# Packing one projection tile into TensorE's column halves, and moving some weight sums to another stage

## The chip, the cores and the metric

The kernel runs on one core of one Trainium2 chip. The metric is the device time of one execution in microseconds (us), as the median of several runs. Below, TensorE (PE in the profile) multiplies, with its weight loads shown as PEld; VectorE is DVE, ScalarE is ACT, GpSimd is POOL, and SyncE is SP, whose queue issues nearly all the transfers of this kernel.

## The reference

One layer of a hybrid encoder: 512 tokens, model width 2048, everything in fp32.

```python
xn = rmsnorm(h, norm_mix)
y  = xn @ w_in                       # 2048 -> 7472 columns
o_gdn  = gdn_group(y[..., :4112])    # 8 heads x 128, gated delta rule
o_rwkv = rwkv_group(y[..., 4112:])   # 16 heads x 64, RWKV-7
h = h + concat([o_gdn, o_rwkv]) @ w_out
h = h + cross_attention(rmsnorm(h), rmsnorm(mem), wq, wk, wv, wo)   # 4 heads, 256 memory tokens
h = h + square(relu(rmsnorm(h) @ w_up)) @ w_down                    # hidden width 8192
out = rmsnorm(h, norm_final)
```

The columns of w_in are mostly whole 128-column tiles. What is left over are small groups: 64 columns for the decay and 64 for the in-context rate of RWKV, 160 for its gate, and 8 + 8 for the decay and the write strength of the delta rule (a_dt and b). Of the gate's 160 columns 128 fill a tile; the other 32 and the 16 of a_dt and b come to 48.

## The kernel before

**Precision.** Most products are made three times at the fast fp32r rate: weight and activation are each split into a high and a low part (a cast on ScalarE, a subtraction on VectorE), and hi x hi, hi x lo and lo x hi are summed in PSUM. Small products of the two recurrences are plain fp32 matmuls, which the hardware runs in two passes; the trace shows each pass as a record.

**The stages.** (1) Projection: 59 tiles of 128 columns of w_in, each 16 blocks of the width, three products a block, 48 matmuls of 128x128 weights on 512 tokens. The raw x (xr) is loaded in 16 blocks into buffers that later serve the recurrences (gq, gk, gAq, gkt and so on), multiplied by the norm's gain and split into xhi and xlo. The division by the root mean square comes at eviction, as a factor rstd for each token: evict multiplies PSUM by rstd into one of four y buffers. Between the tiles the chains of the recurrences (rwkv and gdn, head after head), the memory's keys (kp) and their product with the query weights (kq) run. The products of this last step, KQd, go to DRAM. (2) Values and their product with the output weights (vp, vo). (3) The output projection (op) in a Strassen-like form with seven products for eight. (4) Scores: sixteen steps, two token-by-memory halves g of eight steps n2, each loading 512 KB of KQd into a ring of three buffers (kqr, tag wraw), splitting it (kqh, kql) and multiplying it with hh and hl, 24 matmuls a step. Then attention (at). (5) The MLP's up and down products, in the seven-product form as well.

**The sums.** The seven-product form of the down weights needs four sums of the four quadrants of each block, s1 to s4. They don't depend on the activations, so for 13 of the 16 (e, m) groups they are made beforehand, stored to DRAM (Sd) and later loaded like weights. Each piece is four loads from w_dm, four VectorE operations in place and four stores. presum writes one piece. Eight groups are made during the projection stage in pieces of 410 columns by a chain of low rank (ahead); what is left is made in pieces of 512 or 256 columns (remaining, leftover) during the up and down stages in whatever buffers are free.

**The order.** In stages 1 and 5 the order of every engine is written out by a planner in the kernel: chains (Python generators) yield operations; run() picks the one that can start first by the planner's own clocks (cost, start) with a penalty by the chain's rank, and issues it. A chain can also yield a condition such as after("rstd"); that holds the chain in the planner, not on the chip. cost() holds the estimated time of each form of operation. In the score stage the framework orders the instructions by its own estimate of when they are ready, and adds the semaphores everywhere.

**Where the change touches it.** The third tile, n = 2, holds the 32 gate columns, a_dt, 24 zeros, b and 56 zeros (layout, at the end of the file). Its weights are entries w = 4 and 5 of the list wq, each 512 KB, prepared by loader; projections() multiplies it through gemm_ and hands it to evict; rows() reads it: gate rows 0 to 31, a_dt from row 32, b from row 64, mixes it with the token before (shiftmix), and writes the rows that the delta rule needs into R, then to DRAM as Rd and, transposed, into RT. gdn(h) reads Rd. splits() frees the weight buffers of the two down groups whose sums are made in place.

Of the kernel before, what the change touches and what calls it, by code (L numbers as in the profile page):

```python
# [73 lines left out]
def build(tc, I, out):  # L74
# [136 lines left out]
    def cost(op):  # L211
        eng, nm, _, a, k, out, ins, _ = op
        n = out.free_size()
        if eng == "PE":
            l = ins[0]
            if l.dtype == F32R:
                return n * 0.417 + (13.3 if state["shape"] is None else 120.0)
            sh = (l.partition_size(), l.free_size())
            sw = 0 if state["shape"] == sh or sh == (128, 128) else 100
            if nm == "transpose":  # L220
                return sw + (110 if sh[0] > 64 else 40)
            if sh == (64, 64):
                return sw + (32 if op[5].tensor.name[:2] in ("ri", "gi", "pa", "pv", "pu", "pw", "pk", "po", "pp") else 59)
            if sh[0] < 128 and n == 512:
                return sw + 530
            return sw + (115 if sh[0] < 128 and n == 128 else 2 * max(n * 0.84, 114))
        if eng == "DVE":
            if nm == "memset":
                return 60 + 0.3 * n
            if nm == "tensor_scalar":  # L230
                return 210 + 0.45 * n
            if nm == "tensor_tensor_scan":
                return 90 + 2.2 * n
            return 190 + 1.05 * n if nm == "scalar_tensor_tensor" else 154 + 1.05 * n
        if eng == "ACT":
            need = {AF.Tanh: "e", AF.Ln: "l", AF.Exp: "e"}.get(a[2] if len(a) > 2 else None)
            return (140 + 0.885 * n + 80 * sum(isinstance(x, bass.AP) for x in k.values())
                    + (40 if len(a) > 2 else 0) + (1283 if need and need != state["table"] else 0))
        if eng == "POOL":
            return 116 + 0.75 * n if nm == "memset" else 235 + 2.3 * n  # L240
        return 100.0
# [143 lines left out]
    wq = [("w", I["w_in"][n][:, h * 1024:(h + 1) * 1024]) for h in range(2) for n in range(2)]  # L385
    for n in range(2, NIN):
        wq += [("s", mem4[j]) for j in range(4) if n == NSQ[j]]
        wq += [("w", I["w_in"][n][:, h * 1024:(h + 1) * 1024]) for h in range(2)]
    kpo = [(0, 0), (1, 0), (0, 1), (1, 1)] + [(n, h) for n in range(2, KD) for h in range(2)]
    INSITU = ((3, 0), (3, 1))  # L390
    PRE = ((3, 0, 0),)
# [29 lines left out]
    hk = [("w", I["wk"][n][:, h * 1024:(h + 1) * 1024]) for n, h in kpo]  # L421
    wq += hk[:1] + [("m", m) for m in mem4[:2]] + hk[1:]
    wq += [("w", I["wqT"][n][:, g * 1024:(g + 1) * 1024]) for n in range(KD) for g in range(2)]
    NKP, NKQ = 2 * NIN, 2 * NIN + 2 * KD
    raws, halves, used, whole, piece = {}, {}, set(), set(), {}

    def pieceload(i):
# [10 lines left out]
    def loader():  # L438
        w = nm = 0
        for i, (kind, _) in enumerate(wq):  # L440
            yield lambda: i in raws
            if kind == "w":
                if w in (2, 3):
                    hi, lo = (tile_of(pm, [P, 1024], F32R, t, f"w{t}", 1) for t in ("BK", "AR", "GA", "GB")[2 * w - 4:2 * w - 2])
                else:
                    prev = (w if w < 2 else w - 2) - NWS
                    if prev >= 0:
                        yield lambda: prev + 2 * (prev > 1) in used
                    hi, lo = halves[w] if w in piece else wsplit()
                if w in piece:  # L450
                    yield after("piece", w)
                    yield from split_(raws[i][:, 512:], hi[:, 512:], lo[:, 512:])
                else:
                    yield from split_(raws[i], hi, lo)
                    halves[w] = hi, lo
                whole.add(w)
                w += 1
            else:
                yield from (memory if nm >= 4 else squares)(nm % 4, raws[i])
                nm += 1  # L460
# [88 lines left out]
    def gemm_(pts, his, los, first, nk=KD, left=None):  # L549

        w = len(pts)
        for h in range(nk // 8):
# [15 lines left out]
            for j in range(w):  # L568
                used.add(first + h * w + j)

    khl = []

    def projections():
# [4 lines left out]
        for n in range(2, NIN):  # L578
# [7 lines left out]
            if n >= 4:  # L586
                yield after("py", n - 2)
            pt = psb(f"py{n}", "mm", 2)
            yield from gemm_([pt], xhi, xlo, 2 * n, left="x" if n == NIN - 1 else None)
            chain(evict(n, pt), 0)  # L590
        yield after("py", NIN - 2)
        kpt = {}
# [59 lines left out]
        yield SY.dma_start(KQd[i // 2][:, i % 2 * 512:i % 2 * 512 + 512], ybuf[b][:, 0:512])  # L652
        yfree.append(b)

    def shiftmix(n, mi, o):
        yield after("py", n)
        y = ybuf[ys[n]]
        yield AC.activation(o, y[:, 2:514], AF.Copy, scale=col("mu", mi))
        yield DV.scalar_tensor_tensor(out=o, in0=y[:, 3:515], scalar=omu[:, mi:mi + 1],
                                      in1=o, op0=ALU.mult, op1=ALU.add)  # L660
        yfree.append(ys.pop(n))


# [5 lines left out]
    def rows():  # L669
# [1 line left out]
        yield DV.memset(R, 0.0)  # L671
        rs128 = tl("bon")
        g8 = slice(32, 40)
        b8 = slice(64, 72)
        yield after("rstd")
        yield AC.activation(nA, col("alog"), AF.Exp)
        yield DV.tensor_scalar(out=nA, in0=nA, scalar1=-1.0, scalar2=None, op0=ALU.mult)
# [9 lines left out]
        yield DV.tensor_scalar(out=sg1, in0=sg1, scalar1=0.5, scalar2=0.5, op0=ALU.mult, op1=ALU.add)  # L687
        yield from split_(sg1, sgh, sgl)
        events.add(("lowrank",))
        yield from shiftmix(2, 2, y2)  # L690
        yield AC.activation(y2[0:32, :], y2[0:32, :], AF.Tanh, scale=0.5)
        yield AC.activation(R[b8, :], y2[b8, :], AF.Tanh, scale=0.5)
        yield DV.tensor_scalar(out=y2[0:32, :], in0=y2[0:32, :], scalar1=0.5, scalar2=0.5,
                               op0=ALU.mult, op1=ALU.add)

# [23 lines left out]
        for c in range(4):  # L719
            yield TE.transpose(pt[:, c * P:(c + 1) * P], R[:, c * P:(c + 1) * P], ident)  # L720
        yield SY.dma_start(Rd, R[32:96, :])
        yield DV.tensor_copy(RT, pt.rearrange("p (c a b) -> p c a b", a=4, b=32)[:, :, 1:4, 0:8])

    hA, hB = HALF = slice(0, 64), slice(64, 128)
    solving = []
# [366 lines left out]
    def gdn(h):  # L1092
# [34 lines left out]
        E, B = pre.pop(h) if h else tl("gE"), tl("gqd")  # L1127
        if h == 0:
            yield SL.dma_start(E, Rd[h:h + 1, :].broadcast_to([P, T]))
        yield SL.dma_start(B, Rd[32 + h:33 + h, :].broadcast_to([P, T]))  # L1130
        k_ = yield from conv(0, 1, "gk")
        EG = tl("gEG")
        yield AC.activation(EG, E, AF.Exp)
# [549 lines left out]
    def turned():  # L1683
        g, _, probs = turn.pop(0)
        for e in range(2):
            for mt in range(2):
# [4 lines left out]
                S.copy(phi[kk], pt)  # L1691
                V.tensor_tensor(out=plo[kk], in0=pt, in1=phi[kk].bitcast(F32), op=ALU.subtract)

    for g in range(2):
        banks = (("mm", 2), ("mg", 2), ("mg", 2), ("mm", 2)), (("scr", 1), ("scg", 1), ("mx", 2), ("mx", 2))
        pts = [psb(f"sc{g}_{t}", *banks[g][t]) for t in range(4)]
        for n2 in range(8):
# [3 lines left out]
                nc.sync.dma_start(raw[:, i * 512:(i + 1) * 512], KQd[2 * n2 + i][:, g * 512:(g + 1) * 512])  # L1701
            wh = pw.tile([P, 1024], F32R, tag="whi", name=f"kqh{cnt[0]}", bufs=NWS)
            wl = pw.tile([P, 1024], F32R, tag="wlo", name=f"kql{cnt[0]}", bufs=NWS)
            split(raw, wh, wl)
            if g == 0 and n2 < 6:
                second(2 * n2 + 4)
                second(2 * n2 + 5)
# [15 lines left out]
        if g == 1:  # L1723
            for n in range(2):
                begun.append((psb(f"at{n}", "mg"), *wload(VOd[0][:, :, n * P:(n + 1) * P])))
                attend(*begun[n], 0)
        turn.append((g, pts, []))
        if g == 1:
            for t in range(4):
# [203 lines left out]
    def splits():  # L1933
        for u in units:
            if u[0] == "d" and u[1:3] in INSITU and u[1:] not in PRE:
                for i, w in order_of(u):
                    for x in xs(u):
# [2 lines left out]
                        halves[u, i, x] = hl = yield from take(hfree)  # L1940
                        yield from cut(r, *hl)
                        events.add(("half", u, i, x))
                        if w not in (A11, "s2") and (w != A12 or u == units[-1]):
                            wfree.append(r)
                continue
# [422 lines left out]
def layout(inputs):  # L2368
# [8 lines left out]
    def tiles(w):  # L2377
# [6 lines left out]
    zero = lambda n: np.zeros((D, n), f)  # L2384
    o0 = r0 + 3 * GW
    blocks = [w[:, o0:o0 + 128], w[:, o0 + 128:o0 + 256],
              w[:, o0 + 256:o0 + 288], w[:, 4 * GW:4 * GW + 8], zero(24),
              w[:, 4 * GW + 8:4 * GW + 16], zero(56)]
    for j in range(8):
        s = slice(j * P, (j + 1) * P)  # L2390
        blocks += [w[:, r0:][:, s], w[:, r0 + GW:][:, s], w[:, r0 + 2 * GW:][:, s]]
        blocks += [w[:, i * GW:][:, s] for i in (1, 0, 2, 3)]
    d["w_in"] = tiles(np.concatenate(blocks, 1))

    prm = np.zeros((P, NPRM), f)

# [69 lines left out]
```

## Time and profile before

| | |
|---|---|
| median of 3 runs | 2888.71 us (2887.84 to 2888.92) |
| span of the profiled execution | 2890.0 us; the page gives no other time for it |
| TensorE busy | 2862.2 us, 99% of the span |
| VectorE busy | 2333.9 us, 81% |
| ScalarE busy | 1571.7 us, 54% |
| GpSimd busy | 214.7 us, 7% |
| read from and written to HBM | 443.45 MB and 106.31 MB |

Matmuls are pipelined, so the length of a matmul's record is its latency, not the time that it keeps the array. How long it keeps the array is seen from the start of one to the start of the next. In the views below, a row of the timeline gives the start, the length, the engine, the line of the kernel, the operation, out<-in by the program's names, the form and the count. A row of stages gives the stretch, its length, and for each engine the busy time with the number of instructions in brackets. A row of groups gives the busy time, the mean in ns, and the idle time of the engine before these instructions with what ended it. A row of waits gives who waited for whom, the total in us, how often, and the longest.

### The profile page before, as it was taken

The numbers are of one execution on the slowest core, as the hardware profiler recorded it, in microseconds if no ns is written. First come the engines' busy times: TensorE is split into PE (matmuls) and PEld (weight loads), VectorE is DVE, ScalarE is ACT, GpSimd is POOL, SyncE is SP. The second block draws the span as 40 slices with busy tenths as digits, with TensorE's granted clock in tenths as the row PEclk, the third lists the DMA queues.
The fourth block names the chain that finished last, engine by engine and source line by source line (L and its number), as shares of the span: only waits on it lengthen the run. The fifth ranks groups of instructions, "written<-read, shape, count | busy, mean of one in ns | idle before, by whom it ended". The sixth has DMA issues, their size and how long they took to land.

```text
span 2890.0 us, 49168 instructions
## 1 busy us (share of the span) xinstructions
PE 2862.2 (99%) x18794; PEld 2419.1 (84%) x18794; DVE 2333.9 (81%) x3559; ACT 1571.7 (54%) x2233; POOL 214.7 (7%) x539
## 2 busy tenths in 40 slices
PE   9999999999999999999999999999999999999998
PEld 7877887877877888889988888888888888888887
DVE  7787787787877877769956898899998878786888
ACT  6555555645656655664445556555555644454544
POOL 0213213213212100000000000000000000000000
PEclk9999999999999999999999999999999999999999
DMA  5656656657656788784422354666565878887733
GB/s 191 166 147 176 176 149 187 165 154 189 180 161 200 214 257 274 232 292 151 124 95 88 110 164 153 199 195 207 189 200 178 292 249 277 295 257 247 265 101 110
DMA packets 321212, 553.01 MB, mean 191 GB/s; under 512 B 101128, under 2 KB 188428, under 8 KB 320976
## 3 DMA queue, kind: packets, MB, share of 16 engines
q1 hardware_dynamic: 293584, 518.41, 58.7%
q10 hardware_dynamic: 27392, 31.46, 3.1%
q8 instruction: 147, 2.41, 0.3%
q14 instruction: 89, 0.73, 0.1%
HBM read 443.45 MB, written 106.31 MB: 190 GB/s over the span
## 4 chain that ended last, share of the span: by engine, by line
PE 94%; DMA 3%; DVE 1%; ACT 1%; issue 1%; ACTq 0%; SPq 0%; DVEq 0%
PE py L257 22%; PE mxu L257 12%; PE mgd L257 6%; PE mgu L257 6%; PE mxd L257 6%; PE op L122 6%; PE vp L122 3%; PE mmu L257 3%; PE sc L122 3%; PE at L122 3%; PE scrd L257 3%; PE scgd L257 3%; PE mmd L257 3%; PE kq L257 3%; PE kp L257 2%; DMA wraw<-in_wo 1%
## 5 line engine op out<-in xcount | busy, mean ns | idle before, releaser
L257 ACT CAST whi<-wraw 128x1024 fp32r<-128x1024 f32 (+1 forms) x365 | 382.8, 1049 | 370.1 <-PE py L257 138.7
L257 DVE TENSOR_TENSOR wlo<-wraw,whi 128x1024 fp32r<-128x1024 f32 (+1 forms) x365 | 446.8, 1224 | 90.0 <-ACT whi L257 82.5
L257 PE MATMUL py<-xhi,whi 128*128 128x512 f32 x928 | 373.9, 403 | 6.8 <-ACT xhi L257 6.8
L257 PE MATMUL py<-xhi,wlo 128*128 128x512 f32 x928 | 373.1, 402 | 0.0
L257 PE MATMUL py<-xlo,whi 128*128 128x512 f32 x928 | 372.4, 401 | 0.0
L257 ACT CAST whi<-w 128x1024 fp32r<-128x1024 f32 x178 | 187.6, 1054 | 174.0 <-PE scgd L257 42.3
L257 DVE TENSOR_TENSOR wlo<-w,whi 128x1024 fp32r<-128x1024 f32 x178 | 217.3, 1221 | 43.4 <-ACT whi L257 40.9
L257 PE MATMUL mxu<-cb,whi 128*128 128x512 f32 x1016 | 249.3, 392 | 0.0
L257 PEld LDWEIGHTS mxu<-cb,whi 128*128 128x128 f32 x1016 | 184.7, 189 | 34.3
L257 PEld LDWEIGHTS py<-xhi,whi 128*128 128x128 f32 x928 | 175.3, 189 | 42.0 <-ACT xhi L257 6.8
L257 PEld LDWEIGHTS py<-xhi,wlo 128*128 128x128 f32 x928 | 175.3, 189 | 34.7 <-issue 1.0
L257 PEld LDWEIGHTS py<-xlo,whi 128*128 128x128 f32 x928 | 175.3, 189 | 33.8 <-DVE xlo L257 0.5
L131 DVE TENSOR_TENSOR wlo<-wraw,whi 128x1024 fp32r<-128x1024 f32 x112 | 136.7, 1222 | 44.8 <-ACT whi L130 44.3
L130 ACT CAST whi<-wraw 128x1024 fp32r<-128x1024 f32 x112 | 117.6, 1051 | 86.8 <-PE op L122 26.2
L257 PE MATMUL mxu<-cb,wlo 128*128 128x256 f32 x1016 | 142.7, 283 | 0.7 <-DVE wlo L257 0.7
L257 PEld LDWEIGHTS mxu<-cb,wlo 128*128 128x128 f32 x1016 | 135.1, 191 | 6.0 <-DVE wlo L257 0.9
L257 PE MATMUL mgu<-cb,whi 128*128 128x512 f32 x512 | 129.3, 394 | 0.1
L257 PE MATMUL mxd<-whi,cb 128*128 128x512 f32 x512 | 126.8, 389 | 0.0
L257 PE MATMUL mgd<-whi,cb 128*128 128x512 f32 x512 | 126.4, 389 | 0.0
L257 ACT ACT_TABLE_LOAD x87 | 111.6, 1283 | 16.5 <-DVE suml_gon L257 8.6
L122 PE MATMUL op<-ob,whi 128*128 128x256 f32 (+1 forms) x752 | 115.2, 304 | 0.0
L257 ACT CAST whi<-ws 128x1024 fp32r<-128x1024 f32 x75 | 79.0, 1053 | 64.0 <-PE mgu L257 48.1
(943 smaller groups left out, 6429.3 us busy)
## 6 DMA issues: line engine op xcount, KB each, us to landing
wraw<-in_w_in SPq DMA_DIRECT2D x116, 512.0 KB, 4.7
wraw<-in_w_up SPq DMA_DIRECT2D x65, 512.0 KB, 3.6
w<-in_w_up SPq DMA_DIRECT2D x63, 512.0 KB, 4.2
ds<-in_w_dm SPq DMA_DIRECT2D x128, 205.0 KB, 4.4
sd_s<-ds SPq DMA_DIRECT2D x128, 205.0 KB, 4.9
wraw<-sd_s SPq DMA_DIRECT2D x51, 512.0 KB, 4.9
w<-sd_s SPq DMA_DIRECT2D x50, 512.0 KB, 5.5
w<-in_w_dm SPq DMA_DIRECT2D x48, 512.0 KB, 4.9
```

Of the source, the lines that this page charges most:

```text
L122: PE.matmul(o, l, r, start=start, stop=stop, skip_group_check=again)
L130: S.copy(hi, src)
L131: V.tensor_tensor(out=lo, in0=src, in1=hi.bitcast(F32), op=ALU.subtract)
L257: f(*a, **k)
```

## The change

The third tile is packed into 64 columns: 32 gate columns, a_dt, b, 16 zeros. Its weights for all 16 blocks of the width then fill one 512 KB load instead of two. The weights aren't split: VectorE multiplies them by the norm's gain in fp32, and TensorE multiplies them with the raw x in fp32. Even blocks go to PSUM partitions 0 to 63 and odd blocks to 64 to 127, in pairs; the eviction copies the upper half down, adds and multiplies by rstd. rows() now waits, in the planner, until these products are issued, since it reuses buffers of the raw x. b comes from rows 32 to 47 with a_dt (16 rows are moved), so R's rows 64 to 79 hold both, and Rd and RT are read accordingly.

In the score stage, each of the first 15 steps fetches a piece of 256 columns of the sums that are still open into new buffers (two sets of four), the next step sums it behind its own split, and the step after that stores it before it fetches. What is left then goes to the up and down stages as before. In splits(), the buffer of s1 is handed back only after s2, which reads it, has been issued.

```diff
--- before.py
+++ after.py
@@ cost()
+            if sh == (128, 64) and n == 512:
+                return sw + 440
@@ wq
-        wq += [("w", I["w_in"][n][:, h * 1024:(h + 1) * 1024]) for h in range(2)]
+        wq += [("w", I["w_in"][n][:, h * 1024:(h + 1) * 1024]) for h in range(2 if n > 2 else 1)]
@@ loader()
-                if w in piece:
+                if w == 4:
+                    c = lambda a: a.rearrange("p (k c) -> p k c", c=64)
+                    yield DV.tensor_tensor(out=c(hi.bitcast(F32)), in0=c(raws[i]),
+                                           in1=cols("norm_mix").unsqueeze(2).broadcast_to([P, KD, 64]), op=ALU.mult)
+                    halves[w] = hi, lo
+                elif w in piece:
...
+    def gemm_halves(pt, first):
+
+        yield half(first)
+        yield lambda: len(xhi) == KD
+        w = halves[first][0].bitcast(F32)
+        for k in range(0, KD, 2):
+            yield [TE.matmul(pt[i * 64:i * 64 + 64, :], w[:, (k + i) * 64:(k + i) * 64 + 64], xr[k + i],
+                             start=k == 0, stop=k == KD - 2) for i in (0, 1)]
+        used.add(first)
+        events.add(("few",))
+
+    def evict_halves(n, pt):
+        yield after("rstd")
+        yield lambda: bool(yfree)
+        b = yfree.pop(0)
+        t = short()
+        yield AC.copy(t[0:64, :], pt[64:128, :])
+        yield DV.tensor_tensor(out=t[0:64, :], in0=pt[0:64, :], in1=t[0:64, :], op=ALU.add)
+        yield DV.tensor_tensor(out=ybuf[b][0:64, 3:515], in0=t[0:64, :], in1=rstd[0:64, :], op=ALU.mult)
+        ys[n] = b
+        events.add(("py", n))
...
-            yield from gemm_([pt], xhi, xlo, 2 * n, left="x" if n == NIN - 1 else None)
+            if n == 2:
+                yield from gemm_halves(pt, 4)
+                chain(evict_halves(n, pt), 0)
+                continue
+            yield from gemm_([pt], xhi, xlo, 2 * n - 1, left="x" if n == NIN - 1 else None)
@@ rows()
-        b8 = slice(64, 72)
+        b8 = slice(64, 80)
+        yield after("few")
...
-        yield from shiftmix(2, 2, y2)
+        yield from shiftmix(2, 2, y2, slice(0, 64))
...
-        yield AC.activation(R[b8, :], y2[b8, :], AF.Tanh, scale=0.5)
+        yield AC.activation(R[b8, :], y2[32:48, :], AF.Tanh, scale=0.5)
...
-        yield DV.tensor_copy(RT, pt.rearrange("p (c a b) -> p c a b", a=4, b=32)[:, :, 1:4, 0:8])
+        p4 = pt.rearrange("p (c a b) -> p c a b", a=4, b=32)
+        yield DV.tensor_copy(RT[:, :, 0:3:2, :], p4[:, :, 1:4:2, 0:8])
+        yield DV.tensor_copy(RT[:, :, 1, :], p4[:, :, 2, 8:16])
@@ scores
+    spans = [(e, m, c, min(c + M, 2048)) for e, m in todo for c in range(upto.get((e, m, "s4"), 0), 2048, M)]
+    held, made_ = [], []
+
+    def fetched(s):
+        e, m, c, n = spans.pop(0)
+        b = [pl.tile([P, M], F32, tag=f"ds{i}", name=f"ds{s}_{i}", bufs=2)[:, 0:n - c] for i in range(4)]
+        for i in (A21, A22, A11, A12):
+            nc.sync.dma_start(b[i], I["w_dm"][e, m][i][:, c:n])
+        held.append((e, m, c, n, b))
+
+    def summed():
+        e, m, c, n, (a11, a21, a22, a12) = held.pop(0)
+        for j, o, x, y, op in (("s1", a22, a21, a22, ALU.add), ("s3", a21, a11, a21, ALU.subtract),
+                               ("s2", a11, a22, a11, ALU.subtract), ("s4", a12, a12, a11, ALU.subtract)):
+            V.tensor_tensor(out=o, in0=x, in1=y, op=op)
+            made_.append((Sd[e, m, j][:, c:n], o))
+            upto[e, m, j] = n
+        if n == 2048:
+            todo.remove((e, m))
+
+    def stored():
+        while made_:
+            nc.sync.dma_start(*made_.pop(0))
...
             wl = pw.tile([P, 1024], F32R, tag="wlo", name=f"kql{cnt[0]}", bufs=NWS)
+            stored()
+            if g * 8 + n2 < 15:
+                fetched(g * 8 + n2)
             split(raw, wh, wl)
+            if g * 8 + n2:
+                summed()
...
                 attend(*begun[n], 0)
+            stored()
@@ splits()
                         events.add(("half", u, i, x))
+                        if w == "s1":
+                            yield after("sum", u, "s2", x)
```

More of the change, by code (lines that the diff above doesn't have):

```diff
@@ L423, in build @@
     wq += [("w", I["wqT"][n][:, g * 1024:(g + 1) * 1024]) for n in range(KD) for g in range(2)]
-    NKP, NKQ = 2 * NIN, 2 * NIN + 2 * KD
+    NKP, NKQ = 2 * NIN - 1, 2 * NIN - 1 + 2 * KD
     raws, halves, used, whole, piece = {}, {}, set(), set(), {}
@@ L653, in qevict, with shiftmix @@
         yfree.append(b)
-    def shiftmix(n, mi, o):
+    def shiftmix(n, mi, o, z=slice(0, P)):
         yield after("py", n)
         y = ybuf[ys[n]]
-        yield AC.activation(o, y[:, 2:514], AF.Copy, scale=col("mu", mi))
-        yield DV.scalar_tensor_tensor(out=o, in0=y[:, 3:515], scalar=omu[:, mi:mi + 1],
-                                      in1=o, op0=ALU.mult, op1=ALU.add)
+        yield AC.activation(o[z], y[z, 2:514], AF.Copy, scale=col("mu", mi)[z])
+        yield DV.scalar_tensor_tensor(out=o[z], in0=y[z, 3:515], scalar=omu[z, mi:mi + 1],
+                                      in1=o[z], op0=ALU.mult, op1=ALU.add)
         yfree.append(ys.pop(n))
@@ L1129, in gdn @@
             yield SL.dma_start(E, Rd[h:h + 1, :].broadcast_to([P, T]))
-        yield SL.dma_start(B, Rd[32 + h:33 + h, :].broadcast_to([P, T]))
+        yield SL.dma_start(B, Rd[40 + h:41 + h, :].broadcast_to([P, T]))
         k_ = yield from conv(0, 1, "gk")
@@ L2386, in layout @@
     blocks = [w[:, o0:o0 + 128], w[:, o0 + 128:o0 + 256],
-              w[:, o0 + 256:o0 + 288], w[:, 4 * GW:4 * GW + 8], zero(24),
-              w[:, 4 * GW + 8:4 * GW + 16], zero(56)]
+              zero(128)]
     for j in range(8):
@@ L2393, in layout @@
     d["w_in"] = tiles(np.concatenate(blocks, 1))
+    few = np.concatenate([w[:, o0 + 256:o0 + 288], w[:, 4 * GW:4 * GW + 16], zero(16)], 1)
+    d["w_in"][2, :, 0:1024] = few.reshape(16, P, 64).transpose(1, 0, 2).reshape(P, 1024)
     prm = np.zeros((P, NPRM), f)
```

## The prediction

> **What bounds the kernel.** I read the page first: busy time of each engine and the chain that ended last.
>
> ```profile
> PE 2862.2 (99%) x18794; PEld 2419.1 (84%) x18794; DVE 2333.9 (81%) x3559; ACT 1571.7 (54%) x2233; POOL 214.7 (7%) x539
> ...
> PE 94%; DMA 3%; DVE 1%; ACT 1%; issue 1%; ACTq 0%; SPq 0%; DVEq 0%
> ```
>
> TensorE is named for 94% of the chain. A busy TensorE need not run at its peak, so I next asked for busy time by stage. The stretches are: the third tile (n=2), the rest of the projection stage, the scores, the up stage and the down stage.
>
> ```profile
> core 0: us, PE busy (x) PEld busy (x) DVE busy (x) ACT busy (x) POOL busy (x), PEclk, DMA share, GB/s
> ...
> 32.08:42.96 10.88, 10.88 (x49) 9.01 (x48) 7.12 (x10) 4.73 (x9) 0.00 (x0) 1.00 0.46 152
> 42.96:1117.40 1074.44, 1065.84 (x9274) 867.40 (x9273) 837.36 (x1531) 594.96 (x867) 212.29 (x528) 1.00 0.64 180
> ...
> 1455.40:1545.30 89.90, 89.90 (x410) 74.59 (x409) 37.86 (x62) 32.75 (x55) 0.00 (x0) 1.00 0.31 99
> ...
> 1641.00:2264.00 623.00, 622.21 (x3705) 553.89 (x3704) 560.96 (x743) 353.95 (x494) 0.00 (x0) 1.00 0.59 184
> 2264.00:2875.00 611.00, 611.00 (x2709) 506.38 (x2708) 502.27 (x600) 306.98 (x368) 0.00 (x0) 1.00 0.71 234
> ```
>
> The scores and the down stage have no idle TensorE at all, the up stage 0.8 us. Only the projection stage has some, 8.6 us in 1074, and the view of TensorE's waits in that stretch says where:
>
> ```profile
> PE kp L257 <- DVE wlo L257: 2.7, 1, 2.7
> PE rs L257 <- DVE Qs L257: 2.2, 2, 1.2
> PE gs L257 <- DVE TtG L257: 1.2, 1, 1.2
> PE kq L257 <- DVE y L257: 1.1, 1, 1.1
> ```
>
> So every microsecond of TensorE work taken out should come off the end, and work taken from VectorE or the queues is worth nothing unless it ends one of these few waits.
>
> **Part 1, the third tile: what goes.** The timeline of TensorE around it:
>
> ```profile
> 31.85 0.40 PE L257 MATMUL py<-xhi,wGB 128*128 128x512 f32 x1
> 32.08 0.39 PE L257 MATMUL py<-xhi,whi 128*128 128x512 f32 x1
> ...
> 42.97 0.39 PE L257 MATMUL py<-xhi,whi 128*128 128x512 f32 x1
> 43.19 1.02 PE L257 MATMUL pss<-r,cst 128*128 128x512 f32 x2
> 43.65 0.79 PE L257 MATMUL py<-xlo,whi 128*128 128x512 f32 x1
> 44.28 0.39 PE L257 MATMUL py<-xhi,wlo 128*128 128x512 f32 x1
> ```
>
> Sixteen blocks of three products, 48 matmuls, start at 32.08; the 49th, of the next tile, at 42.97. That is 10.9 us, 0.227 each. All of it goes, with one 512 KB load, two casts and one of two subtractions, none of which TensorE waited for here.
>
> **What comes.** Sixteen fp32 matmuls of 64 columns, in eight pairs: even blocks into PSUM partitions 0 to 63, odd ones into 64 to 127. The price of an fp32 product over 512 columns is in the rows above: pss, the only fp32 one here, starts at 43.19, one ordinary py follows it, and the py after that starts at 44.28. pss therefore held the array from 43.19 to 44.28 - 0.23 = 44.05, that is 0.86 us, two passes of 0.43.
>
> No row shows two column halves under 128 rows. Two rows are near. First, the pair pW and pA, two row halves, also fp32 over 512:
>
> ```profile
> 58.37 0.39 PE L257 MATMUL py<-xlo,whi 128*128 128x512 f32 x1
> 58.69 0.69 PE L257 MATMUL pW<-wa,lw 64*128 64x512 f32 x1
> 58.70 0.69 PE L257 MATMUL pA<-wa,lw 64*128 64x512 f32 x1
> 59.22 0.59 PE L257 MATMUL pW<-wa,lw 64*128 64x512 f32 x1
> ...
> 60.08 0.39 PE L257 MATMUL py<-xhi,whi 128*128 128x512 f32 x1
> ```
>
> The two start 0.01 apart, and the pair holds the array from 58.37 + 0.23 = 58.60 to 60.08 - 0.23 = 59.85: 1.25 us against 1.72 for two in turn. Of it 0.86 are the passes and 0.4 is the change of shape, into it and back. Second, the quadrants: pat takes a row half into one column half, pv the same rows into the other.
>
> ```profile
> 108.64 0.23 PE L257 MATMUL pat<-cst,AR 64*64 64x64 f32 x2
> 108.65 0.23 PE L257 MATMUL pv<-cst,v 64*64 64x64 f32 x2
> 108.69 0.23 PE L257 MATMUL pat<-cst,AR 64*64 64x64 f32 x2
> ...
> 108.94 0.57 PE L257 MATMUL pv<-cst,v 64*64 64x64 f32 x14
> ```
>
> A round of two pat and two pv takes 0.05 to 0.06 us (108.64 to 108.69). The lone pv at the end, with no pat beside them, go two at a time: fourteen in 0.57 less their latency of 0.22, about 0.06 a round again. So the second column half was free, though its rows were streaming for the first. I take pairs side by side: 8 x 0.86 + 0.4 = 7.3 us, a gain of 10.9 - 7.3 = **3.6 us**. The bounds: with no price for the shape change, 6.9 and a gain of 4.0; with the halves in turn, 16 x 0.86 + 0.4 = 14.2 and a loss of 3.3. I am near the first because the quadrant row is the one that has columns in it.
>
> [...]
>
> **The rest of part 1.** The new products read the raw x tiles, so those stay held to about 39.4 (32.08 + 7.3); what reuses them first (the low-rank rows) waits for rstd, which is later:
>
> ```profile
> 46.25 0.63 ACT L257 ACTIVATE rstd<-rstd 128x512 f32<-128x512 f32 x1
> ...
> 46.91 1.89 DVE L257 TENSOR_TENSOR y<-py,rstd 128x512 f32<-128x512 f32 x3 [1.67 <-ACT rstd L257]
> ```
>
> Eviction grows from one VectorE operation to a ScalarE copy and two VectorE operations: 46.91 + 2 x 0.63 for the first two tiles, then about 0.7 + 0.6 + 0.7, so 50.2 at the latest. The bank is wanted by the fifth tile at 32.08 + 7.3 + 0.86 + 10.9 = 51.1. Cost 0; if rstd came 2 us later than before, TensorE would wait 1.1 us once. The two-part copy into RT and the 16-row Tanh add one short VectorE operation off the chain.
>
> **Part 2, the sums.** Fifteen pieces of 256 columns, each four loads, four VectorE sums and four stores, move from the up and down stages into the score stage. Rows that price them, the last being from the tile view of the stores:
>
> ```profile
> L131 DVE TENSOR_TENSOR kql<-kqr,kqh 128x1024 fp32r<-128x1024 f32 x14 | 17.1, 1224 | 39.8 <-ACT kqh L130 39.7
> ...
> L1420 DVE TENSOR_TENSOR h<-h,op 128x256 f32<-128x256 f32 x1 | 0.4, 422 | 0.1
> ```
> ```profile
> SPq L1701 <- DVE kql L131: 61.0, 13, 9.9
> SPq L151 <- DVE kql L131: 16.0, 3, 6.7
> SPq L151 <- DVE wlo L131: 9.7, 2, 4.8
> ```
> ```profile
> DMA to landing us min/median/max: 2.0/4.8/8.7
> ```
>
> VectorE: 60 x 0.42 = 25 us on top of 37.9 busy of 89.9; 39.8 of its idle time lies before kql, where it only waits for ScalarE. SP: 120 issues of about 0.4, 48 us, into a queue that waits 61.0 + 16.0 + 9.7 = 87 us for buffers. Both fit: 0. What they leave is thirty 512-column sums in stages whose TensorE is busy 611.00 of 611.00 and 622.21 of 623.00: a gain between 0 and 0.8; I take 0. The new hold on the s1 buffer is one in the planner's order, not a wait on the chip: the next casts of the in-place units stand behind it, for one subtraction, under the same full TensorE: 0, and about 1 us each if that cover were gone.
>
> The cover for part 2 is the lead of the KQ loads:
>
> ```profile
> L1701 SPq DMA_DIRECT2D kqr<-kqd x27: 319/431/1332, 1440.0 to 1513.6; - x27
> ...
> DMA to landing us min/median/max: 2.8/3.1/4.3
> ```
>
> The last is issued at 1513.6 and lands 3.1 later; its 24 matmuls begin at 1545.3 - 5.4 = 1539.9, so the lead is 23 us.
>
> **The sum.** -3.6 + 0 + 0. The profiled execution's time is its span, 2890.0; the page gives nothing around it, and it lies 1.3 above the runs' median of 2888.7. A difference carries over: 2888.7 - 3.6 = 2885.1.
>
> **Rivals.**
> *Weight loads show.* In the pW rows the second pass starts 0.53 after the first, not 0.43. If every pass of a column pair costs that, the tile takes 16 x 0.53 + 0.2 = 8.7, gain 2.2: 2886.5. [...] Against: the quadrant rounds.
> *Halves in turn:* the packing doesn't do what it says, +3.3: 2892.0. Only a limit that the quadrants don't meet would do it.
> *The order is redrawn, for better.* The projection stage's order comes from the planner's clock, which now runs 3.6 ahead; the stage's 8.6 us of idle may come out otherwise. Without them: 2885.1 - 8.6 = 2876.5; half of them, 2881. For: they are single events, not a pattern. Against: the last heads' chains that cause them remain.
> *The order is redrawn, for worse:* as much again, 2893.7.
> *SP holds up the KQ loads (slower).* A fetch overwrites buffers whose stores were issued just ahead of it, so SP stands until they land. If the next KQ load is queued behind it, a step costs ten issues of 0.43 and a landing of 4.8, 9.1 us, where TensorE takes 89.9 / 16 = 5.6. Thirteen steps (those after the first three buffers) fall 13 x 3.5 = 45 us behind, 23 of them covered: +22, 2907. It decides from a landing of 5.6 + 23/13 - 4.3 = 3.1 us on. For: nothing but the order on SP prevents it. Against: these stores are 128 KB, not the 205 KB of the row, and SP isn't kept in the order of the code here:
>
> ```profile
> 1421.17 0.80 SPq L1701 DMA_DIRECT2D kqr<-kqd  x2
> ...
> 1434.62 3.54 SPq L1613 DMA_DIRECT2D sl<-in_xT  x2
> ```
>
> The x loads come earlier in the code, yet the KQ loads went first, when their buffers were free.
>
> **Chances.** Forecast 0.52; weight loads show 0.12; in turn 0.06; better order 0.13; worse order 0.07; SP 0.10. About 0.2% (5.8 us) is what a measurement of this kernel tells from no change. Faster by more, below 2882.9: most of the better order and the forecast's edge (a microsecond or two of order luck), 0.22. Slower by more, above 2894.5: SP and the tail of the worse order, 0.12. Within: 0.66. The likeliest case's own range is 2882.5 to 2887.5. The range for 8 in 10 runs from 2880, half of the better order, to 2892.5, the halves in turn; SP and the far ends stay out.
>
> **What would show it.** Part 1: TensorE's rows for n=2 read 128*64, start in twos 0.01 apart, and step 0.43; the next tile's first product is at about 39.4, not 42.97. A step of 0.53 or starts 0.43 apart mean the first two rivals. The stage's end (1117.4) should move by the same 3.6; a different shift is the order. Part 2: scores still 89.9 long with VectorE near 63 busy; up and down still 623 and 611. A TensorE wait for kql, or scores longer than 92, would be the SP rival and would prove the forecast wrong, as would an up or down stage shorter by over 1 us.

## The result, and the profile after

The changed kernel takes 2915.08 us (median of 4 runs, 2913.2 to 2918.59), the kernel before 2888.82 (4 runs, the three shown and one more). The ratio is 1.0088, with a 95% interval from 1.0075 to 1.0101: 26 us slower, where 3.6 us faster was forecast.

First the page of the kernel after: busy time of each engine, and the chain that ended last by engine.

```profile
span 2911.4 us, 49285 instructions
...
PE 2865.9 (98%) x18778; PEld 2417.5 (83%) x18778; DVE 2335.9 (80%) x3588; ACT 1567.7 (54%) x2232; POOL 213.0 (7%) x539
...
PE 90%; DMA 5%; DVE 2%; ACT 1%; issue 1%; SPq 1%; POOL 1%; ACTq 0%; DVEq 0%; POOLq 0%
```

TensorE's share of the chain fell from 94 to 90%. By the spans it was idle for 27.8 us before (2890.0 - 2862.2) and for 45.5 after (2911.4 - 2865.9), and its busy time grew by 3.7: most of the new time is waiting. The same five stretches as before, in the kernel after (stretch, its length, busy time of each engine, granted clock, DMA share, GB/s):

```profile
core 0: us, PE busy (x) PEld busy (x) DVE busy (x) ACT busy (x) POOL busy (x), PEclk, DMA share, GB/s
31.44:38.66 7.22, 7.22 (x34) 2.32 (x33) 5.13 (x7) 3.12 (x5) 0.00 (x0) 1.00 0.51 171
38.66:1123.90 1085.24, 1069.37 (x9277) 872.03 (x9278) 833.15 (x1526) 596.01 (x873) 210.55 (x528) 1.00 0.59 174
1461.70:1567.00 105.30, 94.04 (x410) 76.28 (x409) 60.78 (x122) 32.98 (x56) 0.00 (x0) 0.95 0.74 223
1662.70:2285.90 623.20, 622.39 (x3708) 554.20 (x3707) 561.34 (x742) 353.94 (x495) 0.00 (x0) 1.00 0.57 184
2285.90:2896.90 611.00, 611.00 (x2706) 506.25 (x2705) 489.53 (x580) 306.97 (x370) 0.00 (x0) 1.00 0.64 216
```

The third tile is 3.7 us shorter (7.22 against 10.88). The scores are 15.4 longer (105.30 against 89.90): 11.3 of idle TensorE, and 4.1 more busy time for the same matmuls, with a clock of 0.95. Up and down are as long as before. The rest of the projections lost time. The starts of the first matmul of each stage, from the two profiled executions, place it. TensorE's very first product starts at 6.79 us before and at 6.21 after; here and in the experiments, starts of stages are shifted so that it lies at 6.79 in all. (The rows of the scores are cut at these shifted times too, so they lie up to 1.2 us beside the stage's own ends; TensorE's busy time changes by less than 0.1 us by it.)

| first product of | before | after | shift |
|---|---|---|---|
| kp | 907.2 | 903.7 | -3.5 |
| vp | 1118.2 | 1123.9 | +5.7 |
| sc | 1455.3 | 1461.7 | +6.4 |
| at | 1545.2 | 1567.0 | +21.8 |
| the end (last matmul) | 2879.4 | 2901.3 | +21.9 |

So about the tile's gain is there at kp (though the new order has put off 62 of 5050 records of recurrence matmuls until behind it), 9.2 us are lost from there to vp, and 15.4 in the scores. (The spans differ by 21.4, the medians by 26.3: the profiled execution of after is the quickest of its four.)

**The tile.** TensorE's timeline in the kernel after (start, length, operation, shape, count):

```profile
31.21 0.40 PE L259 MATMUL py<-xhi,wGB 128*128 128x512 f32 x1
31.54 0.64 PE L259 MATMUL py<-gq,whi 128*64 128x512 f32 x1
31.54 0.64 PE L259 MATMUL py<-gk,whi 128*64 128x512 f32 x1
32.02 0.59 PE L259 MATMUL py<-gq,whi 128*64 128x512 f32 x1
32.02 0.59 PE L259 MATMUL py<-gk,whi 128*64 128x512 f32 x1
32.45 0.59 PE L259 MATMUL py<-gv,whi 128*64 128x512 f32 x1
32.45 0.59 PE L259 MATMUL py<-gz,whi 128*64 128x512 f32 x1
...
38.03 0.59 PE L259 MATMUL py<-Kt,whi 128*64 128x512 f32 x1
38.55 0.50 PE L259 MATMUL py<-xhi,whi 128*128 128x512 f32 x1
38.89 0.39 PE L259 MATMUL py<-xlo,whi 128*128 128x512 f32 x1
```

The two halves start together and a pass steps 0.43. The price of the shape change is in four steps: into the tile and behind it 0.33 and 0.34 instead of 0.23, and its first and last step 0.48 and 0.52 instead of 0.43, together 0.35.

**The projections.** TensorE's waits in the kernel after, from the tile to vp (who waited for whom, total, count, longest):

```profile
PE ri7s L259 <- DVE k L259: 3.1, 1, 3.1
PE pkk L259 <- DVE gk L259: 2.6, 1, 2.6
PE gi7x L259 <- DVE gk L259: 2.5, 1, 2.5
PE kp L259 <- DVE wlo L259: 2.1, 1, 2.1
PE gi7u L259 <- DVE TtG L259: 1.6, 2, 0.8
```

Before, a few such waits were the 8.6 us of idle (9.1 up to the first vp product). Now it is 15.9 (1085.24 - 1069.37), and the new ones (ri7s, pkk, gi7x) are matmuls of the last heads' recurrences, which stand elsewhere in the planner's new order. The busy time has grown too, by 3.2 us for nearly as many matmuls (1069.37 against 1066.17 up to the first vp product), and the stretches around 1020 show most of why:

```profile
1016.00:1022.00 6.00, 2.37 (x65) 1.85 (x64) 5.30 (x15) 2.31 (x5) 0.00 (x0) 1.00 0.89 245
1022.00:1026.00 4.00, 2.65 (x25) 2.28 (x26) 1.50 (x5) 0.00 (x0) 0.00 (x0) 0.50 0.42 157
1026.00:1030.00 4.00, 4.00 (x16) 3.37 (x17) 0.87 (x3) 0.00 (x0) 0.00 (x0) 0.65 0.00 0
```

After 3.6 us of idle TensorE the granted clock is 0.50, then 0.65: 4 x 0.50 + 4 x 0.35 = 3.4 us of clock withheld, of which the busy TensorE could have used 2.65 x 0.50 + 4 x 0.35 = 2.7.

**The scores.** In the kernel after, SP's waits in this stage, the KQ loads by the tile view, TensorE's timeline and VectorE's timeline:

```profile
SPq L1737 <- DMA sd_s<-ds: 21.0, 18, 2.3
SPq L1752 <- DVE ds L1744: 13.3, 21, 6.6
...
SPq L1761 <- DVE kql L131: 1.6, 1, 1.6
```
```profile
L1761 SPq DMA_DIRECT2D kqr<-kqd x32: 320/424/748, 1427.0 to 1545.0; - x32
```
```profile
1529.70 1.03 PE L1725 MATMUL ptr<-cst,pr 128*128 128x128 f32 x8
...
1533.56 0.40 PE L122 MATMUL sc<-kqh,hl 128*128 128x512 f32 x1
1542.75 1.97 PE L1725 MATMUL ptr<-cst,pr 128*128 128x128 f32 x8 [8.79 <-DVE plo L1728]
...
1545.37 0.63 PE L122 MATMUL sc<-kqh,hl 128*128 128x512 f32 x1
1545.80 0.63 PE L122 MATMUL sc<-kqh,hh 128*128 128x512 f32 x1
```
```profile
1531.25 1.22 DVE L131 TENSOR_TENSOR kql<-kqr,kqh 128x1024 fp32r<-128x1024 f32 x1 [3.73 <-ACT kqh L130]
1533.48 0.42 DVE L1744 TENSOR_TENSOR ds<-ds,ds 128x256 f32<-128x256 f32 x1 [1.01 <-DMA ds<-in_w_dm]
1534.16 1.35 DVE L1744 TENSOR_TENSOR ds<-ds,ds 128x256 f32<-128x256 f32 x3 [0.25 <-DMA ds<-in_w_dm]
1537.18 1.22 DVE L131 TENSOR_TENSOR kql<-kqr,kqh 128x1024 fp32r<-128x1024 f32 x1 [1.68 <-ACT kqh L130]
1539.83 1.44 DVE L1744 TENSOR_TENSOR ds<-ds,ds 128x256 f32<-128x256 f32 x3 [1.42 <-DMA ds<-in_w_dm]
1541.66 0.43 DVE L1744 TENSOR_TENSOR ds<-ds,ds 128x256 f32<-128x256 f32 x1 [0.40 <-DMA ds<-in_w_dm]
1542.01 1.28 DVE L1728 TENSOR_TENSOR plo<-ptr,phi 128x512 fp32r<-128x512 f32 x2
```

Before, SP stood 61.0 us for kql, that is, it had time to spare. Now a KQ load waits for kql once, and SP stands 18 times for stores to land (the waits of its fetches, line 1737) and 21 times for a sum that it is to store (line 1752). The last KQ load is issued 83.9 us after the first product (1545.0 - 1461.1, both unshifted), where it was 58.3 (1513.6 - 1455.3). Of these 25.6 us, 13.4 are there at the sixth of the sixteen loads, when a store has stood 6.6 us for the first sum; the other ten add 1.2 each. The KQ loads themselves take little longer to land (a median of 3.4 us in this stage against 3.1), so it is when they are issued that counts. What this makes late is read backwards from TensorE's wait. The second set of transposes needs a bank that plo evicts. The transposes that plo reads were done at 1529.70 + 1.03 = 1530.7, but in VectorE's order two splits and their sums stand ahead of it: the splits come late, since their KQ loads did, and the sums wait for their own fetches. plo runs at 1542.01. And again the clock is half behind the wait of 8.8 us (0.50 from 1540 to 1546): the last two products step 0.43 instead of 0.23.

### The profile page after: what moved, and what is told of

The parts are those of the page before. It is cut to its first block, busy times and chain, and to the rows that moved or that the text cites. A ratio compares the mean times of both kernels' runs of the same rounds, so it can differ in the third digit from the quotient of the medians.

```text
span 2911.4 us, 49285 instructions
## 1 busy us (share of the span) xinstructions
PE 2865.9 (98%) x18778; PEld 2417.5 (83%) x18778; DVE 2335.9 (80%) x3588; ACT 1567.7 (54%) x2232; POOL 213.0 (7%) x539
## 4 chain that ended last, share of the span: by engine, by line
PE 90%; DMA 5%; DVE 2%; ACT 1%; issue 1%; SPq 1%; POOL 1%; ACTq 0%; DVEq 0%; POOLq 0%
PE py L259 21%; PE mxu L259 12%; PE mgd L259 6%; PE mgu L259 6%; PE mxd L259 6%; PE op L122 5%; PE vp L122 3%; PE mmu L259 3%; PE at L122 3%; PE scrd L259 3%; PE scgd L259 3%; PE mmd L259 3%; PE kq L259 3%; PE kp L259 3%; DMA sd_s<-ds 1%; DMA wraw<-in_wo 1%
## 5 line engine op out<-in xcount | busy, mean ns | idle before, releaser
L259 PE MATMUL py<-xhi,whi 128*128 128x512 f32 x912 | 366.4, 402 | 6.2 <-ACT xhi L259 6.2
L259 PE MATMUL py<-xhi,wlo 128*128 128x512 f32 x912 | 365.8, 401 | 0.0
L131 DVE TENSOR_TENSOR wlo<-wraw,whi 128x1024 fp32r<-128x1024 f32 x112 | 136.6, 1221 | 42.9 <-ACT whi L130 42.4
```

Of the source, the lines that this page charges most:

```text
L131: V.tensor_tensor(out=lo, in0=src, in1=hi.bitcast(F32), op=ALU.subtract)
L259: f(*a, **k)
```

## The experiments

The stage lengths below are from the first sc product to the first at product (scores) and from the first down product of the seven-product form to the last matmul (down), taken like the starts above; before they are 89.9 and 532.9, after 105.3 and 532.9.

**1. One part at a time.** The reading so far: part 1's order costs the projections, part 2's transfers in SP's queue cost the scores.

```diff
@@ e1_tile_only
-            stored()
-            if g * 8 + n2 < 15:
-                fetched(g * 8 + n2)
             split(raw, wh, wl)
-            if g * 8 + n2:
-                summed()
@@ e2_sums_only: the kernel before, with these lines, their functions and the hold in splits() added
```

> Only the packed tile; the score stage has no sums (they all stay in the up and down stages). Queue theory: the score stage's 15.4 us came from the sums' place in SP's queue, so scores are back at 89.9 us and the kernel takes 2888.8 + 6.4 = 2895. Order theory: the 6.4 us lost up to the scores stay, with the projection stage again ending near 1124. Rival (the packed tile also harms later stages, through a longer tail or more weight sums left for the MLP): above 2898. Rival (the projection stage's loss came from the sums too, through another order): 2885.

> Only the sums in the score stage; the third tile as before. Queue theory: the projection stage is as before (values begin at 1118), scores take 105 us, and the kernel 2888.8 + 15.4 = 2904. Rival (the late start of the score loads after the packed tile made the queue matter): scores under 95, kernel under 2894.

The tile alone: 2914.19 us, ratio 1.0077 (1.0060 to 1.0095). vp starts at 1125.5, 7 us late; the scores are 89.9 again. But it isn't 2895, since the down stage takes 546.2, 13.3 longer: the time and the mechanism of the rival by which the tile harms later stages, with more sums left for the MLP. TensorE's timeline there:

```profile
2746.46 1.07 PE L259 MATMUL mmd<-wlo,cb 128*128 128x512 f32 x4
2757.05 2.07 PE L259 MATMUL scrd<-whi,cb 128*128 128x512 f32 x4 [9.52 <-ACT whi L259]
```

The redrawn order makes fewer sums in the projections. The tile view of their stores, before and then in the tile alone (148 in the whole change too):

```profile
L257 SPq DMA_DIRECT2D sd_s<-ds x160: 319/328/1158, 106.6 to 1041.7; - x160
```
```profile
L259 SPq DMA_DIRECT2D sd_s<-ds x148: 319/326/1487, 83.1 to 1023.3; - x148
```

More is left for the down stage, and near its end a weight comes late: the cast of whi stands 14.9 us for a load from Sd, which SP issues at 2748.3, right behind the last stores of these sums (2741.4 to 2745.4). In the whole change part 2 hides that: it makes 15 pieces in the scores. The sums alone: 2900.47 us, ratio 1.0033 (1.0022 to 1.0044), a little under the expectation. vp isn't late (1114.9), and the scores take 99.7: 9.8 more, without any tile.

**2. Another order.** The planner prices one narrow product at 440 ns. With another figure the computation is the same, and the order comes out otherwise.

```diff
@@ e4_planner_600, and e12_tile_560 with 560; e5 and e12 without the sums, as in e1
-                return sw + 440
+                return sw + 600
```

> As the changed kernel; only the planner's figure for one packed product is 600 ns instead of 440, which nothing on the chip reads. Order theory: the projection stage gets another order and values begin near 1115 (1118.2 less the 3.6 of the tile), the kernel takes 2915 - 9 = 2906. Rival (the earlier end of the tile itself or its products cost the recurrences their place, whatever the order): values still begin at 1122 to 1125, kernel 2915.

> The change's narrow tile alone, the sums left in the later stages, with the planner's figure for one narrow product set to 600 ns instead of 440. Theory A (what the tile alone lost with 440 was the redrawn order: 8 us in the projection stage and, because fewer sums were made there, 13 us in the down stage): with 600 the planner makes all eight groups of sums again, so the first vp product starts at 1114.5 to 1118 us (before 1118.2), the scores take 90 us, the down stage 533 us, and the ratio to before is 0.9988 to 1.000. Theory B (the down stage was held up because the score stage made no sums, whatever the order): the down stage takes 546 us again and the ratio is about 1.003 to 1.004.

> The narrow tile alone, the sums left in the later stages, with the planner's figure at 560 ns. With the overcharge taken out, the planner's own clock at the end of the projections stands at 1083.1 us for 560 and 1083.0 for 600, against 1086.9 for the kernel before and 1089.1 for 440. Theory A (the order is what the tile's gain hangs on): projections 3 to 5 us earlier than before in the trace, scores 90 us, down stage 533 us, ratio to before 0.9985 to 1.0000, the lower end if TensorE's clock stays whole after the waits of the kp stage. Theory B (the tile costs something of its own, whatever the order): ratio above 1.001.

With 600 the whole change takes 2904.02, ratio 1.0042 (1.0031 to 1.0054): vp at 1117.8, scores 102.0. Without the sums, 600 gives 1.0001 (0.9992 to 1.0011) and 560 gives 0.9998 (0.9990 to 1.0007), with scores of 89.9 and down stages of 532.9; 160 stores are back in the projections. So of the tile alone's 1.0077 all hung on the order that the figure 440 drew. The planner's own clock had it: with the difference between the figure and the measured step of 0.43 taken out for 16 products, its end of the projections is at 1083.1 us for 560 and 1083.0 for 600, against 1089.1 for 440 and 1086.9 before.

The 3.6 us didn't show in the time even so, and a single execution can't show them: e2, which has the order of before in this stage, starts vp 3.3 earlier than before does. But nine of the kept traces follow the order of 600 up to vp (560 draws the same, but for close neighbours), and each records the granted clock, so they can be sorted by how long TensorE had only half of it before vp (the labels are those of the runs here and below):

| order, executions | at half the clock | first product of vp |
|---|---|---|
| 600: e9, e5 | 0 | 1111.1, 1111.7 |
| 600: e7, e8 | 3.4 us | 1115.7, 1116.1 |
| 600 or 560: e13, e12, e4, e10, e11 | 6.4 to 6.8 us | 1116.9, 1117.3, 1117.8, 1118.2, 1119.6 |
| before: e2, before | 0 | 1114.9, 1118.2 |

With a whole clock the new order is 3 to 7 us ahead of that of before; with half the clock for some 6.8 us it is about level. Over all runs the mean granted clock is 0.9979 (600) and 0.9982 (560) against 0.9988 and 0.9986 of the kernel before beside them: 0.0004 to 0.0009 of 2890 is 1 to 3 us. So the tile's gain is there, and by its size the clock takes most of it back. Why this order loses the clock more often isn't shown; its idle time before vp (7.1 to 11.7 us) is not much longer than in the two executions of before's order (9.1 and 6.7).

**3. Transfers or VectorE?** On the tile with the figure 600, where the later stages make all the sums, one half of part 2's work at a time is added to the scores, with results that nobody reads: the 60 fetches and 60 stores (into spare DRAM) without the sums, or the 60 sums (on tiles that stay in SBUF) without the transfers.

```diff
@@ e7_transfers: summed()
-            V.tensor_tensor(out=o, in0=x, in1=y, op=op)
-            made_.append((Sd[e, m, j][:, c:n], o))
+            made_.append((spare[s * 4 + i][:, c:n], b[i]))
@@ e8_adds: the loop
-            stored()
-            if g * 8 + n2 < 15:
-                fetched(g * 8 + n2)
```

> The tile with the figure 600; in the score stage only the transfers of the change are kept (60 fetches, and 60 stores into spare DRAM), its 60 additions and subtractions are left out, and the later stages make the sums themselves as before. Queue theory (SP's issues, and its standing until stores have landed, hold up the KQ loads): first score product to first at product 99 to 103 us, as with the whole change (102.0), and TensorE waits several us for plo at the transposes. Rival (the 25 us of VectorE work are in the way): 90 to 92 us.

> The tile with the figure 600; in the score stage only the 60 additions and subtractions of the change are kept, on tiles that stay in SBUF, its transfers are left out, and the later stages make the sums themselves as before. Queue theory: first score product to first at product 90 to 92 us. Rival (VectorE work in the way): 96 to 102 us.

One run of each: 2899.91 us with the transfers alone and 2892.43 with the sums alone, against a median of 2890.66 of the kernel before beside them. The scores, transfers alone and then sums alone:

```profile
1453.50:1552.10 98.60, 92.68 (x415) 76.53 (x414) 37.88 (x61) 32.17 (x50) 0.00 (x0) 0.97 0.75 230
```
```profile
1455.60:1545.40 89.80, 89.80 (x411) 74.58 (x411) 59.53 (x123) 33.90 (x56) 0.00 (x0) 1.00 0.32 103
```

The sums cost nothing, with VectorE busy 59.5 us, as the prediction had it; the transfers cost 8.7, with VectorE as idle as before, and TensorE waits 5.9 for plo. Two limits: sums that wait for no fetch are moved forward by the framework (they start 1.1 to 36.8 us after the first product, where those of the whole change with 600 go on to 84.0), so sums beside the transposes aren't tested; and the whole change loses 12.1 with this figure, so some 3.4 come only of both together, which fits sums that stand for their fetch. The KQ loads of the transfers kernel:

```profile
L1757 SPq DMA_DIRECT2D kqr<-kqd x32: 319/420/427, 1420.6 to 1530.9; - x32
```

Over the last eight of them SP comes round every 6.7 us (6.5 in the whole change), where a step's 24 products take TensorE 5.45. The last is issued 76.2 us after the first product (1530.9 - 1454.7, both unshifted), 17.9 later than before; the stage is 8.7 longer. In the whole change the same two numbers are 25.6 and 15.4. So 9 to 10 us of lateness are absorbed, in both.

**4. Standing, issues, or another queue.** Three ways to relieve SP.

```diff
@@ e3_three_sets: the whole change, figure 440
-        b = [pl.tile([P, M], F32, tag=f"ds{i}", name=f"ds{s}_{i}", bufs=2)[:, 0:n - c] for i in range(4)]
+        b = [pl.tile([P, M], F32, tag=f"ds{i}", name=f"ds{s}_{i}", bufs=3)[:, 0:n - c] for i in range(4)]
@@ e11_one_fetch: figure 600
-        for i in (A21, A22, A11, A12):
-            nc.sync.dma_start(b[i], I["w_dm"][e, m][i][:, c:n])
+        nc.sync.dma_start(t[:, :, 0:n - c], I["w_dm"][e, m][:, :, c:n].rearrange("i p c -> p i c"))
@@ e9_pool_queue: figure 600
-            nc.sync.dma_start(b[i], I["w_dm"][e, m][i][:, c:n])
+            nc.gpsimd.dma_start(b[i], I["w_dm"][e, m][i][:, c:n])
-            nc.sync.dma_start(*made_.pop(0))
+            nc.gpsimd.dma_start(*made_.pop(0))
```

> As the changed kernel, with three sets of fetch buffers instead of two, so that a fetch no longer follows the stores of the same buffers at once; issues, bytes and VectorE work are the same (one probability tile moves to another pool for the room). Queue theory (SP stands 1.7 us a step for the landing of stores): a step needs 4.6 us of SP, under the 5.6 of TensorE; scores 90 to 93, kernel about 2900. Contention theory (the added VectorE sums, transfers and issues slow the step): scores stay at 105, kernel 2915.

> The whole change with the figure 600 and all fifteen steps, the four quadrants of a piece fetched by one DMA instead of four, so that SP issues 7 transfers a step instead of 10, with the same bytes, stores and sums. Issue theory (an issue takes SP about 0.43 us, so a step falls from 6.6 to 5.3 us, under TensorE's 5.4): 90 to 93 us from the first score product to the first at product, ratio to before 0.999 to 1.001. Rival (SP stands for the stores' landing and the transfers' time, whatever the number of issues): 98 to 102 us and a ratio of 1.003 to 1.004.

> The whole change with the figure 600, the fetches and stores of the sums in the score stage issued by GpSimd instead of SP, so that SP's queue holds the KQ loads alone. Queue theory: 90 to 94 us from the first score product to the first at product instead of 102.0, ratio to before 0.999 to 1.001. Rival (VectorE's order: additions that stand in the stream wait for their fetch or fill it): 98 to 102 us and a ratio of about 1.003 to 1.004.

Three sets: 1.0060 (1.0043 to 1.0077), scores 96.9, between the two theories. SP no longer stands for stores to land, and the KQ loads then come every 5.8 us, close to TensorE's pace, but twelve fetches instead of eight go ahead of the fourth KQ load, and plo is still 5.0 us late. One fetch for four: 1.0056 (1.0040 to 1.0071), scores 101.6. It does relieve SP, whose last KQ load comes 69.6 us after the first product instead of 81.1 with four, but the loss stays: the fetch of 512 KB lands after 4.5 us (four of 128 KB after 2.7 in the kernel with four), and VectorE stands for it. GpSimd's queue: 1.0096 (1.0081 to 1.0111), scores 119.2, worse than the rival said. SP's queue holds only the KQ loads there, a fetch lands after 3.6 us instead of 2.7, and VectorE stands longest of all. VectorE's waits, one fetch and then GpSimd's queue:

```profile
DVE ds L1744 <- DMA ds<-in_w_dm: 19.6, 6, 4.7
```
```profile
DVE ds L1744 <- DMA ds<-in_w_dm: 37.7, 17, 6.3
```

So there are two ways into the same loss: the KQ load behind the pieces in SP's order, and kql and plo behind the sums in VectorE's order. What both hang on, as I read it, is the round of a piece through two sets of buffers: fetch, land, sum, store, land. That isn't shown by itself: three sets loosen the round and still lose 7.0 us.

**5. Fewer steps.** If each step with sums is only a little too long, a few of them should cost nothing, wherever they stand.

```diff
@@ e10_nine_steps
-            if g * 8 + n2 < 15:
+            if g * 8 + n2 < 9:
-            if g * 8 + n2:
+            if 0 < g * 8 + n2 < 10:
@@ e13_late_nine
-            if g * 8 + n2 < 15:
+            if 6 <= g * 8 + n2 < 15:
-            if g * 8 + n2:
+            if g * 8 + n2 > 6:
```

> The whole change with the figure 600, but sums in the first nine of the score stage's sixteen steps instead of fifteen. Lead theory (each step with sums takes SP about 6.6 us against TensorE's 5.4, and the three buffers of KQ loads that lie ahead are used up after some ten to twelve steps): nine steps cost nothing, first score product to first at product 90 to 91 us instead of 102.0, ratio to before 0.999 to 1.0005. Rival (each step with sums costs its share, 12.1 us over 15): 97 us and a ratio of about 1.002.

> The whole change with the figure 600, sums in nine steps again, but in the last nine of the fifteen (pieces fetched in steps 6 to 14) instead of the first nine, so that they stand around the transposes. Lead theory (three buffers of KQ loads are ahead when the sums begin, and nine steps that are each some 1.1 us too long use up less than that): 90 to 92 us from the first score product to the first at product. Place theory (in VectorE's order the sums that wait for their fetch stand ahead of the evictions that the transposes wait for, whatever the lead): 97 to 102 us, with TensorE waiting 5 us or more for plo.

The scores, the first nine steps and then the last nine:

```profile
1457.30:1547.20 89.90, 89.90 (x415) 74.82 (x414) 51.40 (x94) 32.23 (x50) 0.00 (x0) 1.00 0.60 192
```
```profile
1453.90:1543.80 89.90, 89.90 (x409) 74.59 (x409) 50.70 (x98) 32.62 (x56) 0.00 (x0) 1.00 0.62 192
```

Both cost nothing: 1.0000 (0.9991 to 1.0009) and 1.0003 (0.9992 to 1.0014). But the second doesn't test the place at the transposes. The framework moves its pieces forward: the fetches begin 14.8 us before the first score product, as in the first, and the last sum starts 55.6 us behind that product (42.9 in the first, 84.0 with fifteen steps), ahead of both sets of transposes, at 66.3 and 69.4. Whether sums beside the transposes cost something by themselves stays open.

Nor do nine steps draw 9 x 1.2 = 11 us on a store of 10, as the lead theory would have it. Against before, each counted from the first score product, the KQ loads of the first nine steps are 10.9 us late already at the sixth load, 15.7 at the tenth, and not late at all at the last; those of the last nine are never more than 5.5 late. What the two share is that the loads have nearly caught up at the fourteenth of sixteen: 2.5 and 3.8 us late, against 12.3 with the transfers alone and 17.2 with all fifteen steps (figure 600). That fits pieces that are free as long as SP has time to catch up before TensorE needs plo. No version tried is faster than the kernel before by more than the interval.

## Why the prediction was wrong, and where it was right

**The tile's price: right.** 7.2 us against 7.3, a gain of 3.7 against 3.6, starts together, steps of 0.43, a shape change of 0.35 against 0.4. The quadrant rows were the right neighbour, and the rival by which weight loads show, with steps of 0.53 and a tile of 8.7 us, isn't borne out. The eviction at no cost was right too: no wait of the fifth tile shows.

**"Every microsecond of TensorE work taken out should come off the end": wrong.** It was about true up to kp. The step that failed is the order, which entered the sum with nothing and cost 9.2 us between kp and vp (over the whole stretch, some 7 of new waits and about 3 of clock). It is the order and not the tile, since the same tile in the order of 600 or 560 costs nothing; there its gain shows where the clock stays whole. The rival of a worse order had the size of the idle about right (8.6 us more in its sum) with a chance of 0.07. It lacked two things. The order also decides how many sums are made early, and so what the down stage has to do: 13.3 us in the tile alone. And a wait cost more than its length here, by the clock: around 1020 some 2.7 us beside 3.6 of idle TensorE, in the scores 4.1 beside 11.3.

**"Both fit: 0": wrong, and it is the larger part.** 25 us of VectorE work did fit, as the sums alone show (made early, and with no fetch to wait for). 48 us of issues into 87 us of waiting did not: the sum over a stage said nothing about the length of one step, which is a chain. The SP rival (0.10) named this chain, and the reason it gives, fetches that stand for stores to land, is the first row of SP's waits; the second, 13.3 us of stores that stand for their sum, it didn't have. Its sizes were off: each stand was 1.2 us (21.0 / 18), since the landing (3.5 us) runs beside the other issues, and a step took 6.5 to 6.7, not 9.1. The lead was about 10 us, not 23: it was read from the last load to that load's own products, but plo, behind earlier splits in VectorE's order, ran out first. The loss came to 15.4, not 22, and 4.1 of it is the clock. The two reasons against it fell: at 128 KB a landing was still 3.5 us, above the 3.1 from which it was to decide, and SP's order put fetches ahead of the KQ loads after all.

**Up and down: right for the whole change** (623.2 and 611.0), by luck in part: work that part 1's order had added was taken away by part 2.

## What to carry to other kernels

Where a planner writes the order from a table of costs, a shorter operation is also a new order: look at the planner's own end of the stage, and at what else it moves out of the stage, before counting the gain. Work added to a queue that has time to spare is priced by the length of one step of the loop, with every stand for a landing or for a result in it, by how late the first steps already start, and by how much lateness the buffers ahead can take; spare time summed over the stage doesn't answer that. And where a framework orders the instructions, look in the trace where moved work has landed before reading an experiment by its place in the code.

## What the hardware showed that was not expected

The clock fell after a wait of less than 2 us. In the whole change with the figure 600, TensorE waited for 1.95 us (912.02 to 913.97) and had a clock of 0.54 in the next stretch:

```profile
910.00:915.00 5.00, 3.05 (x25) 2.55 (x27) 2.02 (x3) 2.16 (x4) 0.00 (x0) 1.00 0.81 292
915.00:920.00 5.00, 4.40 (x42) 3.45 (x43) 4.23 (x7) 2.48 (x4) 0.00 (x0) 0.54 0.60 205
```

The kernel before waited longer at the same place, 2.71 us (912.93 to 915.64), and kept its clock:

```profile
910.00:915.00 5.00, 2.94 (x18) 2.40 (x16) 1.50 (x4) 1.71 (x3) 0.00 (x0) 1.00 0.93 332
915.00:920.00 5.00, 4.27 (x54) 3.53 (x54) 5.00 (x9) 3.27 (x7) 0.00 (x0) 1.00 0.54 155
```

The records of the clock show where the two differ. In the kernels before and after it is whole or half (1.00 or 0.50) and nothing between: before it is whole until 2883.61, after it is half from 1021.94 to 1028.77 and from 1537.35 to 1547.59, which is 2 and 3 times 3.413 us, with 149 times between them. I cut both executions into stretches of this length (from 20 to 2875 us), with the boundaries on the recorded changes. In the two stretches with a whole clock that were followed by half the clock, TensorE was idle for 1.99 and 3.40 us; in those that were followed by a whole one, for 1.67 at most (1.53 in the kernel before). The wait of 2.71 is cut by a boundary at 914.12 into 1.19 and 1.52. The wait of 1.95 isn't, by an estimate from its rows: 0.54 and 0.77 are 4.6 and 2.3 us at half the clock, so the half began at about 915.4, and the stretch ahead of it, from about 912.0, holds the whole wait. Why the clock follows such stretches isn't shown.
